# One SBUF operand in the small VectorE operations of softmax and norm, and other places for the second eviction tiles, in a two-layer streaming encoder

## The chip, the core and the metric

The kernel runs on one core of a Trainium2 chip. Its engines are TensorE (PE, matmuls, with weight loads as PEld), VectorE (DVE), ScalarE (ACT), GpSimd (POOL) and SyncE (SP), from whose queue all DMAs are issued. The metric is the device time of one execution in microseconds; lower is better. Before the change it is 2810.72 us, the median of three runs (2810.69 to 2818.3).

## The reference

One inference step of a two-layer encoder over 1152 rows of width 1024: a prompt of 1024 positions and 8 samples of 16. Layer 0 uses sliding-window attention with grouped keys, a learned sink per head and a relative-position bias; layer 1 uses chunk-band attention with keys and values shared by all B layers. Cut to what the change touches:

```python
# attention of layer 0, with sinks: the sink joins the maximum and the sum
m = jnp.maximum(s.max(-1, keepdims=True), sink)
e = jnp.exp(s - m)
p = e / (e.sum(-1, keepdims=True) + jnp.exp(sink - m))
o = jnp.einsum('bkgqs,bskd->bqkgd', p.astype(v.dtype), v)
...
# after the attention and after the channel mixer of each layer
x = layer_norm(DEEPNORM_ALPHA * x + (1 + g_m) * mix, ln_g[l, 0], ln_b[l, 0])
f, conv_rows = conv_ffn(h, ...)          # causal convolution, GEGLU, down-projection
x = layer_norm(DEEPNORM_ALPHA * x + (1 + g_f) * f, ln_g[l, 1], ln_b[l, 1])
...
def layer_norm(x, g, b):
    mu = x.mean(-1, keepdims=True)
    var = jnp.square(x - mu).mean(-1, keepdims=True)
    return (x - mu) * lax.rsqrt(var + LN_EPS) * g + b
```

## The kernel before, in words

Matmul operands are kept as a high and a low part (fp32r), so a product takes three passes; `split` (line 167 the cast on ACT, line 178 the subtraction on DVE or POOL) makes the two parts. The rows stand as 9 token tiles of 128 (tile 8 holds the samples). The program is: `opening`, `attention(0)`, `out_proj(0)`, `ffn(0)` with `down`, then the same for layer 1, whose attention begins with `kv`. A scheduler sets the order of the instructions on each engine from the order in which the program writes them and its own timeline; within an engine they then run strictly in that order. Waits between engines are on semaphores, derived from which parts of a tile are written and read.

The large SBUF tile F is used again and again: in each stage an arena hands out pieces of it. In `attention(0)` these are, by column, the softmax results (7328 to 9888), the bias tiles (to 10400), the transposed weights `pTs` of the sample items (10400 to 10784), `osm`, `rl`, then `L` (11040, the sums of the exponentials), `M` (11168, the negated maxima), `ost` and `pitem` (from 11808). At the same time the K and V projections of the attention's start still use F for the second eviction tiles: `kstore` and `vtile` evict a result once as high and low part into X2 and, for the last rows that are outputs, once more in plain form into a tile of the ring `kvt`, 384 columns each, from which a DMA stores it (line 371 for V). Before the change these tiles lie at 10368, 10752, 11136, 11520, 11904 and 12288. V is computed for the token tiles 0, 1, 2, 8, 3, 4, 5, 6, 7 in this order; tile 7 gets the ring's third tile, at 11136.

For each head and pair of query tiles, `scores` lets PE form the scores (lines 540 and 543) and `softmax` adds the bias and takes the minimum of the negated scores with an accumulator output in `M` (line 507, on DVE), then exponentiates on ACT with the sum into `L` (line 511). `weigh` transposes the weights on PE (568), `sums` adds the sink's share to `L` and inverts (lines 612 to 614), `values` multiplies with V (590) and `normalise` scales on POOL (628). Between them lie the query projections (296), pieces of the adaLN projections (224, with weights loaded by line 216), and the sample items: scores (682), a softmax that adds the sink's share in line 699, transposes (708), values (717), a scaling on DVE (725) and a transpose back (730). Near the end, `ocast` and `woload` put splits of 1024 columns on ACT and POOL (lines 167 and 178).

In the norms, `rsqrt` refines the inverse root by a Newton step: lines 967, 968 and 969 are operations on one column of 128 rows. `norm_tail` closes the first three norms, and POOL multiplies by the gain there (line 1039). `norm_last` closes the last one: for token tiles in `VT` two operations on DVE apply mean, gain, root and shift (993, 994); for the others ACT applies mean and root (996, 997), POOL the gain (998) and DVE the shift (999). In the last stage the tiles are finished in the order 0, 1, 2, 6, 7, 8, 3, 4, 5, so tile 5 is the last of the program.

## Time and profile before

| | us |
|---|---|
| median of three runs | 2810.72 |
| profiled execution | 2808.31 |
| its span, from the first to the last instruction | 2806.5 |
| PE busy in the span | 2701.0 |
| DVE busy | 1898.8 |
| ACT busy | 1307.8 |
| POOL busy | 1117.7 |
| mean granted TensorE clock | 0.987 |

The first attention lies from about 84 to 390 us of the span, its output projection until about 500, the channel mixer of layer 0 and its norm until about 1270, K, V and the attention of layer 1 from there to about 1900, and the last channel mixer ends the program. In a timeline row the columns are start in us, length in us (of all the instructions merged in the row), engine, line, operation, out<-in, and in brackets the idle time before it with what ended it. In a row of stretches each engine has its busy time and its count in the order PE, PEld, DVE, ACT, POOL, and then come the granted TensorE clock (1.00 is full), the share of DMA time and GB/s. SPq is the DMA queue on SyncE: the length there is that of issuing.

### The profile page before, as it was taken

What the parts mean: (1) busy time and instruction counts of PE and PEld (TensorE: products, weight loads), DVE (VectorE), ACT (ScalarE), POOL (GpSimd) and SP (SyncE); (2) the same over time, 40 slices, a digit from 0 to 9 for tenths busy, and PEclk for the clock granted to TensorE, in tenths of its full rate; (3) what the DMA queues carried; (4) which work ended last, traced back from release to release, by engine and by line L of the source; (5) the groups of instructions that cost most, each with busy time, mean ns of one, the idle gap of its engine ahead of it and who ended that gap; (6) DMA issues with size and microseconds to landing.
All of it is one profiled execution on the core that took longest, in us unless ns stands there. A gap on an engine that the chain in (4) does not pass through costs nothing.

```text
span 2806.5 us, 46569 instructions
## 1 busy us (share of the span) xinstructions
PE 2701.0 (96%) x17398; PEld 2384.3 (85%) x17398; DVE 1898.8 (68%) x3622; ACT 1307.8 (47%) x2607; POOL 1117.7 (40%) x755
## 2 busy tenths in 40 slices
PE   7999889999999999999999999989999999999997
PEld 5897768989999998777898888867899999998886
DVE  4376768776666684766854667766887777774764
ACT  3375633533333343443536666663444444444442
POOL 2132523444333457565220121242444333458662
PEclk9999999999999999999999999999999999999999
DMA  7656434474444446665757457763432222247662
GB/s 291 212 157 198 146 98 173 146 250 142 143 156 145 142 132 220 214 225 195 266 199 268 120 153 192 221 202 122 170 123 71 72 80 71 71 143 256 210 199 76
DMA packets 205187, 467.96 MB, mean 167 GB/s; under 512 B 34752, under 2 KB 97936, under 8 KB 204960
## 3 DMA queue, kind: packets, MB, share of 16 engines
q1 hardware_dynamic: 204960, 464.98, 51.0%
q8 instruction: 137, 2.24, 0.3%
q14 instruction: 90, 0.74, 0.1%
HBM read 365.17 MB, written 109.17 MB: 169 GB/s over the span
## 4 chain that ended last, share of the span: by engine, by line
PE 40%; DVE 4%; DMA 3%; ACT 2%; issue 1%; POOL 0%; SPq 0%; POOLq 0%; DVEq 0%; ACTq 0%
PE PS L1203 18%; PE PS L1386 10%; PE PS L296 4%; PE PS L309 4%; PE PS L590 1%; PE PS L568 1%; PE PS L540 1%; DVE F L507 1%; DMA F<-hmD 1%; PE PS L543 1%; ACT F L919 1%; PE PS L717 0%; DVE wl L178 0%; DMA F<-hD 0%; DVE xa L178 0%
## 5 line engine op out<-in xcount | busy, mean ns | idle before, releaser
L1203 PE MATMUL PS<-H,wh 128*128 128x320 f32 (+1 forms) x2752 | 427.9, 298 | 0.0
L1203 PEld LDWEIGHTS PS<-H,wh 128*128 128x128 f32 x2752 | 390.3, 192 | 0.4 <-issue 0.4
L1164 DVE TENSOR_TENSOR F<-PS,F 128x256 f32<-128x256 f32 (+1 forms) x446 | 197.7, 453 | 199.7 <-PE PS L1203 198.9
L167 ACT CAST wh<-F 128x512 fp32r<-128x512 f32 (+3 forms) x265 | 168.0, 645 | 328.3 <-PE PS L1203 186.6
L1379 DVE TENSOR_TENSOR xa<-xa 128x384 fp32r<-128x384 f32 x132 | 180.8, 1379 | 190.5 <-ACT xa L167 189.0
L1250 DVE SCALAR_TENSOR_TENSOR F<-F 128x1024 f32<-128x1024 f32 x320 | 258.9, 855 | 4.5 <-ACT F L1289 3.4
L178 DVE TENSOR_TENSOR wl<-F,wh 128x512 fp32r<-128x512 f32 (+2 forms) x236 | 215.0, 924 | 61.9 <-ACT wh L167 61.5
L1203 PE MATMUL PS<-H,wl 128*128 128x320 f32 (+1 forms) x1376 | 244.0, 300 | 8.7 <-ACT F L1171 7.2
L296 PE MATMUL PS<-H,wh 128*128 128x384 f32 (+1 forms) x1152 | 225.1, 339 | 0.0
L1386 PE MATMUL PS<-wh,xa 128*128 128x512 f32 x696 | 222.0, 395 | 0.0
L178 POOL TENSOR_TENSOR wl<-ws,wh 128x1024 fp32r<-128x1024 f32 x59 | 148.6, 2523 | 178.8 <-ACT wh L167 144.1
L1203 PEld LDWEIGHTS PS<-H,wl 128*128 128x128 f32 x1376 | 205.1, 192 | 16.9 <-ACT F L1171 7.7
L1203 PE MATMUL PS<-xa,wh 128*128 128x320 f32 (+1 forms) x1408 | 216.6, 296 | 1.4 <-DVE xa L178 1.4
L167 ACT CAST wh<-ws 128x512 fp32r<-128x512 f32 (+1 forms) x159 | 126.8, 804 | 190.8 <-PE PS L1203 94.8
L296 PEld LDWEIGHTS PS<-H,wh 128*128 128x128 f32 x1152 | 200.9, 189 | 1.3 <-issue 0.8
L1203 PEld LDWEIGHTS PS<-xa,wh 128*128 128x128 f32 x1408 | 197.4, 189 | 2.1 <-DVE xa L178 1.7
L1259 POOL TENSOR_TENSOR F<-F 128x16 f32<-128x16 f32 x88 | 47.8, 543 | 312.4 <-DVE F L1250 220.5
L1386 PEld LDWEIGHTS PS<-wh,xa 128*128 128x128 f32 x696 | 130.6, 188 | 30.7
L167 ACT CAST xa<-xa 128x384 fp32r<-128x384 f32 x132 | 67.4, 513 | 187.6 <-DMA xa<-actD 181.9
L309 PE MATMUL PS<-wh,H 128*128 128x512 f32 (+1 forms) x576 | 145.7, 367 | 1.4 <-DVE F L1095 0.8
L628 POOL TENSOR_TENSOR F<-F,X 64x512 f32<-64x512 f32 x62 | 79.5, 1282 | 169.6 <-DVE F L604 147.7
L1297 POOL TENSOR_TENSOR F<-F 128x1152 f32<-128x1152 f32 x44 | 119.8, 2722 | 49.5 <-DVE F L1250 31.3
(269 smaller groups left out, 6193.0 us busy)
## 6 DMA issues: line engine op xcount, KB each, us to landing
ws<-in_wdn_dram SPq DMA_DIRECT2D x66, 512.0 KB
F<-in_wdn_dram SPq DMA_DIRECT2D x66, 512.0 KB
ws<-in_adaw_dram SPq DMA_DIRECT2D x64, 512.0 KB
actD<-F SPq DMA_DIRECT2D x44, 576.0 KB
xa<-actD SPq DMA_DIRECT2D x132, 192.0 KB
ws<-in_wup_dram SPq DMA_DIRECT2D x49, 512.0 KB
F<-in_adaw_dram SPq DMA_DIRECT2D x48, 512.0 KB
F<-in_wup_dram SPq DMA_DIRECT2D x39, 512.0 KB
```

Source lines behind the costliest of these rows:

```text
L167: nc.scalar.copy(out, in_)
L178: self.eng(el).tensor_sub(lo, src, hi.bitcast(F32))
L296: mm = self.nc.tensor.matmul(out[:, 0:n], w[a][:, k * 128 : k * 128 + 128], H[:, p, k, s0 : s0 + n], start=i == 0, stop=i == 23)
L309: self.nc.tensor.matmul(out[:, 0:n], H[:, p, j * kn + k, t0 : t0 + 128], w[a][:, k * n : k * n + n], start=i == 0, stop=i == 23,)
L628: self.eng("v" if last else "p").tensor_mul(on[r, q], on[r, q], rb[r, :])
L1164: nc.vector.tensor_add(d, v(ps), a if len(a.shape) == 3 else v(a))
L1203: self.pairmm = nc.tensor.matmul(ps[:, 0:m], w[a][:, k * 128 : k * 128 + 128], x(p, k, n), start=start and c == 0, stop=c == 11, skip_grou ...
L1250: nc.vector.scalar_tensor_tensor(o, u, cw[:, cc, i : i + 1], o, op0=ALU.mult, op1=ALU.add)
L1259: nc.gpsimd.tensor_add(y3[:, :, 0:2], y3[:, :, 0:2], E4[:, cc])
L1297: nc.gpsimd.tensor_mul(yg, yg, ya)
L1379: nc.vector.tensor_sub(lo, raw, hi.bitcast(F32))
L1386: self.downmm = nc.tensor.matmul(ps, a[p][:, i * 128 : i * 128 + 128], w[q][:, hf * 512 : hf * 512 + 512], start=j == 0 and c == 0, stop=j ...
```

## The change

`M` and the part of `L` that takes the sums become one tile `LM` with two columns per query tile, the sum and the negated maximum side by side. `sums` reduces each such pair into `L` with one tensor_reduce, which has one SBUF operand, where it added two tiles. In the sample items' softmax and in `rsqrt` and `norm_last`, products and sums of two columns are written as tensor_scalar: one tensor operand and one column as a scalar per row. The second eviction tiles get fixed places: 9120, 9504, 11520, 11904, 12288 and 10400, in the ring's order. Token tile 5 joins `VT`. No other line changes, but two lines more in the file put the lines after 412 one or two further down: line 507 is 508 then, 613 is 615, 699 is 701, 969 is 971, and 993 to 999 are 995 to 1001.

```diff
-VT = (0, 3, 6, 7)
+VT = (0, 3, 5, 6, 7)
...
         L = fa.take(128)
-        M = sa.take(128) if l == 0 else None
+        LM = fa.take(256).rearrange("p (i t) -> p i t", t=2) if l == 0 else None
...
-        ka = Arena(self.F, 10368 if l == 0 else 0)
-        kvt = Ring([(self.X2[:, i * 768 : i * 768 + 768], ka.take(384)) for i in (0, 3, 1, 4, 2, 5)])
+        late = (9120, 9504, 11520, 11904, 12288, 10400)
+        late = [self.F[:, o : o + 384] if l == 0 else None for o in late]
+        kvt = Ring([(self.X2[:, i * 768 : i * 768 + 768], f) for i, f in zip((0, 3, 1, 4, 2, 5), late)])
...
-                nm = M[:, i : i + 1] if l == 0 else self.sm.next()[:, 0:1]
-                softmax(pieces, p, n, self.sink[:, h : h + 1] if l == 0 else None, nm, L[:, i : i + 1])
+                nm = LM[:, i, 1:2] if l == 0 else self.sm.next()[:, 0:1]
+                rs = LM[:, i, 0:1] if l == 0 else L[:, i : i + 1]
+                softmax(pieces, p, n, self.sink[:, h : h + 1] if l == 0 else None, nm, rs)
...
             if l == 0:
-                nc.scalar.activation(M[:, cs], M[:, cs], AF.Exp, bias=self.sinkH[:, hh : hh + 1])
-                nc.vector.tensor_add(L[:, cs], L[:, cs], M[:, cs])
+                nc.scalar.activation(LM[:, cs, 1], LM[:, cs, 1], AF.Exp, bias=self.sinkH[:, hh : hh + 1])
+                nc.vector.tensor_reduce(out=L[:, cs], in_=LM[:, cs, :], op=ALU.add, axis=mybir.AxisListType.X)
             nc.vector.reciprocal(L[:, cs], L[:, cs])
...
                 nc.scalar.activation(e, sink, AF.Exp, bias=nm, scale=-1.0)
-                nc.vector.tensor_add(rs, rs, e)
+                nc.vector.tensor_scalar_add(rs, rs, e)
             nc.vector.reciprocal(rs, rs)
...
         nc.vector.tensor_scalar(t, t, -0.5, 1.5, op0=ALU.mult, op1=ALU.add)
-        nc.vector.tensor_mul(r, r, t)
+        nc.vector.tensor_scalar_mul(r, r, t)
...
         else:
-            nc.vector.tensor_mul(m, s, r)
+            nc.vector.tensor_scalar_mul(m, s, r)
```

What stands on DVE at the first softmax of the program, before (PS is PSUM, F, C and xa are SBUF tiles, DMAHW0 to 7 the semaphores of the DMA queue; the rows of line 494 are the low parts of the query projection):

```order
L494 SCALAR_TENSOR_TENSOR xa<-PS,xa 64x256 [waits PE_49,Activation_49]
L507 ISA F<-PS,F,C 128x128 [waits DMAHW0_49,DMAHW1_49,PE_49,Pool_49]
L507 ISA F 128x1
L494 SCALAR_TENSOR_TENSOR xa<-PS,xa 64x256 [waits Activation_49]
L507 ISA F<-PS,F,C 128x256 [waits PE_49,Pool_49]
```

And after:

```order
L495 SCALAR_TENSOR_TENSOR xa<-PS,xa 64x256 [waits PE_49,Activation_49]
L508 ISA F<-PS,F,C 128x128 [waits DMAHW0_49,PE_49,Pool_49]
L508 ISA F 128x1
L495 SCALAR_TENSOR_TENSOR xa<-PS,xa 64x256 [waits Activation_49]
L508 ISA F<-PS,F,C 128x256 [waits PE_49,Pool_49]
```

The order is the same; the first softmax no longer waits for one of its two DMAs.

In the attention the small operations keep their places and waits. On DVE, a piece near the end of the first attention (lines 699 and 700 the sample items' sum and inverse, 739 their eviction, 613 and 614 those of the prompt), before:

```order
L699 TENSOR_TENSOR C<-C 128x1 [waits Activation_49]
L739 COPY F<-PS 64x4x16 [waits PE_49]
L739 COPY F<-PS 64x4x16
L613 TENSOR_TENSOR F<-F 128x4 [waits DVE_49,Activation_49]
L700 RECIPROCAL C<-C 128x1 [waits DVE_49]
```

And after:

```order
L701 TENSOR_SCALAR C<-C 128x1 [waits Activation_49]
L741 COPY F<-PS 64x4x16 [waits PE_49]
L741 COPY F<-PS 64x4x16
L615 TENSOR_REDUCE F<-F 128x4 [waits DVE_49,Activation_49]
L702 RECIPROCAL C<-C 128x1 [waits DVE_49]
```

Only the form of two rows differs: one tensor operand, where there were two.

The last rows of DVE, the norm of token tile 5, before (986 and 990 prepare mean and variance, 965 to 969 the inverse root):

```order
L990 TENSOR_SCALAR C<-C 128x1 [waits Activation_49]
L965 RECIPROCAL C<-C 128x1 [waits Activation_49]
L967 TENSOR_SCALAR C<-C 128x1 [waits DVE_49]
L968 TENSOR_SCALAR C<-C 128x1 [waits DVE_49]
L969 TENSOR_TENSOR C<-C 128x1 [waits DVE_49]
L996 TENSOR_TENSOR C<-C 128x1 [waits DVE_49]
L999 TENSOR_TENSOR F<-F 128x1024 [waits Pool_49]
```

And after:

```order
L992 TENSOR_SCALAR C<-C 128x1 [waits Activation_49]
L995 SCALAR_TENSOR_TENSOR F<-F,C 128x1024 [waits DVE_49]
L967 RECIPROCAL C<-C 128x1 [waits Activation_49]
L969 TENSOR_SCALAR C<-C 128x1 [waits DVE_49]
L970 TENSOR_SCALAR C<-C 128x1 [waits DVE_49]
L971 TENSOR_SCALAR C<-C 128x1 [waits DVE_49]
L996 SCALAR_TENSOR_TENSOR F<-F,C 128x1024 [waits DVE_49]
```

The wait for POOL at the end is gone, and with it one operation of 1024 columns on ACT and one on POOL; DVE has two in place of one, the first of them ahead of the inverse root. Elsewhere the scheduler exchanges some neighbours: on all engines at the starts of the two channel mixers and in `kv`, a few matmuls in the output projections.

## Prediction

> **What bounds the kernel now.** I read the page's busy times and chain first, then the waits of VectorE (DVE) by line over the first attention, then the timeline wherever TensorE (PE) stands idle in it, with the granted clock beside it.

> ```profile
> PE 2701.0 (96%) x17398; PEld 2384.3 (85%) x17398; DVE 1898.8 (68%) x3622; ACT 1307.8 (47%) x2607; POOL 1117.7 (40%) x755
> PE 40%; DVE 4%; DMA 3%; ACT 2%; issue 1%; POOL 0%; SPq 0%; POOLq 0%; DVEq 0%; ACTq 0%
> ```

> PE is busy for 96% of the span and carries most of the chain that is traced. So a change on DVE is worth only what it takes out of PE's idle time, or out of time at a lower clock, or out of the end, after the last matmul. Elsewhere it is free. The edit touches three kinds of places.

> **Part 1: the eviction tiles.** Waits of DVE and timelines of the DMA queue, DVE and PE where the first softmax stands (columns: start in us, length in us, engine, line, then in brackets the idle time before and what ended it), and two stretches with the clock (the number before the DMA share):

> ```profile
> DVE F L507 <- DMA out_va_dram<-F: 6.1, 1, 6.1
> ...
> 99.91 0.53 SPq L366 DMA_DIRECT2D vH<-X  x1
> 100.90 0.34 SPq L371 DMA_DIRECT2D out_va_dram<-F  x1
> 106.79 1.00 SPq L471 DMA_DIRECT2D xa<-vH  x2
> 107.88 2.00 SPq L216 DMA_DIRECT2D ws<-in_adaw_dram  x2
> ...
> 100.72 0.42 DVE L494 SCALAR_TENSOR_TENSOR xa<-PS,xa 64x256 fp32r<-64x256 f32 x1 [2.26 <-ACT xa L493]
> 107.26 0.35 DVE L507 CUSTOM_DVE_ANT_0 F<-PS,F,C 128x128 f32<-128x128 f32 x1 [6.12 <-DMA out_va_dram<-F]
> ...
> 107.67 0.38 PE L540 MATMUL PS<-xa 128*128 128x256 f32 x1 [2.73 <-DVE F L507]
> 110.91 0.58 PE L540 MATMUL PS<-xa 128*128 128x256 f32 x1 [1.16 <-DVE F L507]
> ...
> 110.00:117.00 7.00, 6.09 (x22) 6.09 (x23) 4.39 (x17) 4.21 (x15) 0.00 (x0) 0.51 0.70 229
> 117.00:120.00 3.00, 3.00 (x22) 3.00 (x21) 0.75 (x3) 0.78 (x3) 0.00 (x0) 1.00 0.00 0
> ```

> Column 0 of M, the first thing that the first softmax writes, lay at F 11168, inside the tile 11136 to 11392 that holds the V rows of token tile 7 until they are stored. DVE therefore stood 6.12 us for that store. After the change the tile is at 11520 and the wait is gone from the row of the instruction. DVE can go on when L494 ends, at 101.14. PE loses its waits of 2.73 and 1.16, together 3.9 us. Behind the idle time the clock was 0.51 for 7 us. PE was busy 6.09 us of that, so a full clock would give 6.09 x 0.49 = 3.0; I take 2.6, as part of it is short dependent matmuls. What is late next: the V load of L471 still leaves at 106.79, because it reads what the store at 99.91 writes, and the loads of L216 stand behind it in the same queue. All of them have landed by 117 (DMA share 0.00 from there), so PE, 6.5 us earlier, may meet the second one; I take off 1.0. The tiles' new places also overlap pitem and pTs, but these are first used by the items (L699 below, from 189.4), long after the stores. Part 1: 3.9 + 2.6 - 1.0 = 5.5 us, between 0 (all given back to those loads) and 7.

> **Part 2: the small operations.** Rows by line (shortest, median and longest in ns), a control in the norms, and the end of the first attention:

> ```profile
> L613 DVE TENSOR_TENSOR F<-F x32: 140/164/2321, 115.1 to 371.7; 128x4 f32<-128x4 f32 x32
> L699 DVE TENSOR_TENSOR C<-C x16: 128/159/3328, 189.4 to 385.0; 128x1 f32<-128x1 f32 x16
> L969 DVE TENSOR_TENSOR C<-C x36: 104/160/2374, 415.2 to 2797.5; 128x1 f32<-128x1 f32 x36
> L968 DVE TENSOR_SCALAR C<-C x36: 129/153/156, 415.0 to 2797.3; 128x1 f32<-128x1 f32 x36
> L614 DVE RECIPROCAL F<-F x64: 155/178/180, 115.3 to 1887.0; 128x4 f32<-128x4 f32 x64
> ...
> 437.81 2.38 POOL L1039 TENSOR_TENSOR F<-F 128x1024 f32<-128x1024 f32 x1 [11.02 <-DVE C L965]
> 438.31 0.26 DVE L967 TENSOR_SCALAR C<-C 128x1 f32<-128x1 f32 x1
> 438.61 0.15 DVE L968 TENSOR_SCALAR C<-C 128x1 f32<-128x1 f32 x1
> 438.80 1.42 DVE L969 TENSOR_TENSOR C<-C 128x1 f32<-128x1 f32 x1
> 410.00:440.00 30.00, 30.00 (x140) 24.57 (x139) 28.65 (x60) 6.15 (x15) 8.99 (x4) 1.00 0.34 123
> ...
> 329.20 2.34 POOL L178 TENSOR_TENSOR H<-H 128x1024 fp32r<-128x1024 f32 x1
> 328.22 3.33 DVE L699 TENSOR_TENSOR C<-C 128x1 f32<-128x1 f32 x1
> 331.48 0.33 DVE L725 TENSOR_SCALAR F<-PS,C 128x128 f32<-128x128 f32 x1
> 331.87 0.46 PE L730 MATMUL PS<-C,F 128*128 128x128 f32 x1 [3.04 <-DVE F L725]
> 332.00:349.00 17.00, 14.20 (x89) 10.29 (x89) 13.01 (x39) 11.29 (x29) 10.89 (x8) 0.60 0.16 54
> ...
> 290.68 2.32 DVE L613 TENSOR_TENSOR F<-F 128x4 f32<-128x4 f32 x1 [0.21 <-ACT F L612]
> 288.00:295.00 7.00, 7.00 (x55) 6.65 (x48) 6.54 (x15) 6.49 (x18) 3.69 (x2) 1.00 0.46 133
> ```

> The same operation takes 160 ns or up to 3328 ns. At 437.81 GpSimd (POOL) begins a multiply of 2.38 us. Two operations with one SBUF tensor, L967 and L968, run inside it at their usual 0.26 and 0.15 us; L969, with two SBUF operands, ends at 440.22, where the multiply ends (440.19). So it is the second SBUF operand that waits for POOL. The new forms have one: L699 and L969 become the form of L968 (150 ns, never above 156), L613 a reduction that no row shows. By its neighbours it lies between L614's 178 ns on the same four columns and, as an end far away, the 3328 ns above; I take 0.18 us, the nearest row.

> [...]

> What it is worth: L699 at 328.22 loses 3.33 - 0.16 = 3.2 us, L725 behind it starts that much earlier, and with it PE's 3.04. In the 17 us behind, the clock is 0.60 with PE busy for 14.20, which holds 14.20 x 0.40 = 5.7 us; DVE is busy for 13.01 of the same stretch, so I take half, 2.9. Some small idle gaps of PE there belong to later waits of the same two lines; I put 1.1 on those. Part 2 in the attention: 7 us, between 3 (the 3.04 alone) and 11 (the whole 5.7 and 2 more). [...]

> I cost the rest at nothing: L613's 2.32 at 290.68 lies beside a PE that is busy for 7.00 of 7.00, L969's beside 30.00 of 30.00. That cover is PE work in front of the waiting result; if it were gone, each would show its own one or two microseconds. L996 was short each time. The extra cost of the new forms, some 20 ns each, is below what matters.

> **Part 3: token tile 5 in VT.** It is the last tile of the program. Tile 3, already on the other branch, shows what it will do:

> ```profile
> 2778.90 0.15 DVE L990 TENSOR_SCALAR C<-C 128x1 f32<-128x1 f32 x1 [1.31 <-ACT F L989]
> 2778.97 1.28 DVE L993 SCALAR_TENSOR_TENSOR F<-F,C 128x1024 f32<-128x1024 f32 x1
> 2781.05 1.28 DVE L994 SCALAR_TENSOR_TENSOR F<-F,C 128x1024 f32<-128x1024 f32 x1
> ...
> 2796.39 0.15 DVE L990 TENSOR_SCALAR C<-C 128x1 f32<-128x1 f32 x1 [1.31 <-ACT F L989]
> 2797.96 1.24 ACT L997 ACTIVATE F<-F,C 128x1024 f32<-128x1024 f32 x1 [1.18 <-DVE C L996]
> 2799.28 2.34 POOL L998 TENSOR_TENSOR F<-F 128x1024 f32<-128x1024 f32 x1 [6.93 <-ACT F L997]
> 2801.65 1.23 DVE L999 TENSOR_TENSOR F<-F 128x1024 f32<-128x1024 f32 x1 [3.79 <-POOL F L998]
> ```

> From L990 to the end of the row: 2802.88 - 2796.39 = 6.49 us before; in tile 3, 2782.33 - 2778.90 = 3.43. The first of the two operations lies beside the square root, and nothing else is left on DVE. Part 3: 3.0 us, between 2.5 and 3.1. The store of the last row follows as before.

> **Sum.** 5.5 + 7 + 3.0 = 15.5 us. The profiled execution took 2808.31 us (2806.5 of it the span), so 2792.8; the median of the runs shown, 2810.72, stands 2.4 above it, so 2795.2 on that scale. I say 2794. The bounds add up to 5.5 and 21, that is about 2787 to 2805.

> **Rivals.**

> Given back. PE's start in the attention moves, but the next thing in line was late anyway: the weight loads of L216, V of L471, or, at the end, the reloads and normalisations that run through SyncE's queue. For it, the waits of PE from 100 to 400 us:

> ```profile
> PE PS L224 <- DMA ws<-in_adaw_dram: 7.1, 7, 1.3
> ```

> Against: the queue's rows shift with PE, since those loads wait for buffers that PE frees. Then part 3 and about a third of the rest stay: 2808.3 - 7 = 2801.

> The small forms wait all the same. The control row speaks against it for L699 and L969, nothing does for the reduction. Then parts 1 and 3 are left: 2808.3 - 8.5 = 2800.

> The tile is moved in vain: the first softmax meets another transfer, such as its bias, in place of the store. Against it, POOL's fill of the first bias tile had its load at 99.61:

> ```profile
> 99.61 0.14 POOL L520 MEMSET F<- 64x64 f32 x1 [17.10 <-DMA F<-ska]
> ```

> Parts 2 and 3: 2798.

> Slower: the reduction is dear. It stands 32 times in the attention, each in front of the reciprocal and a later softmax. If it costs 1.0 us in place of 0.18 on PE's path, 32 x 0.82 = 26 us are added: 2808.3 - 15.5 + 26 = 2819. It decides from some 0.75 us each, where the saving is used up and 8 more are lost. For it only that no row shows the form; against it the nearest row, L614's 178 ns. [...]

> **How the numbers follow.** Forecast 0.60; given back 0.17; forms wait 0.10; moved in vain 0.07; slower 0.06. What a measurement can tell from no change is 0.3%, 8.4 us: faster means below 2802.3. The forecast and the vain move lie there (0.67), half of the cases at 2800 and 2801 just so, with the 2 us between the two scales in mind (0.05 of 0.10 and 0.05 of 0.17). Faster 0.77, within 0.17, slower 0.06. The range reaches from 2783, the bounds with a little more clock, to 2806, where part 3 alone is left and what was given back is nearly all.

> **What would show it.** Part 1: the first softmax (L508 then) starts near 101, with no wait for the V store, and the clock stays at 1.00 from 110 to 117. Part 2: none of L615, L701, L971 is longer than 0.3 us; the matmul of L732 waits no 3 us; the clock between 325 and 345 has less time at one half. Part 3: the last operation of DVE is the second of two of 1.28 us, 3.4 us behind L992. The forecast is wrong if PE's idle time in the attention is the same as before in sum, at other lines, or if the starts of the channel mixers, where the casts on ScalarE (ACT) stand in a slightly different order now, hold PE up longer than this wait, the longest one from 2050 to 2080 us:

> ```profile
> PE PS L1203 <- ACT F L1171: 4.3, 1, 4.3
> ```

## The result, and the profile after

| | before | after |
|---|---|---|
| median, us (6 runs each, side by side) | 2810.94 (2808.1 to 2818.3) | 2794.45 (2791.05 to 2801.12) |
| ratio of the two | | 0.9938, 95% interval 0.9921 to 0.9956 |
| profiled execution, us | 2808.31 | 2793.26 |
| its span, us | 2806.5 | 2791.5 |
| mean granted clock in it | 0.987 | 0.989 |

The kernel is 16.5 us faster in the medians and 17.4 by the ratio, with an interval of 12 to 22; the forecast was 2794. In a second comparison on another occasion (the run `all_again` below) the same kernel was 10.1 us faster by the ratio, 6.7 to 13.8. That difference matters for what follows: the forecast met the time, but its three terms did not all hold, and the experiments tell which.

The page of the changed kernel, busy time and the chain's shares:

```profile
PE 2696.8 (97%) x17398; PEld 2382.1 (85%) x17398; DVE 1898.6 (68%) x3622; ACT 1305.3 (47%) x2606; POOL 1112.6 (40%) x754
PE 41%; DVE 4%; DMA 3%; ACT 2%; issue 1%; SPq 0%; POOL 0%; DVEq 0%; ACTq 0%; POOLq 0%
```

PE bounds the kernel as before. Its busy time fell by 4.2 us though it executes the same 17398 matmuls, and the time at half clock, summed over the span from the windows in the trace's record of the clock, fell from 71.6 to 62.5 us.

The first softmax, from the timeline of the changed kernel, and the stretch with the clock that was 0.51 before:

```profile
101.06 0.35 DVE L508 CUSTOM_DVE_ANT_0 F<-PS,F,C 128x128 f32<-128x128 f32 x1
110.00:117.00 7.00, 7.00 (x57) 5.89 (x56) 4.49 (x17) 4.19 (x15) 0.29 (x2) 1.00 0.51 183
```

The small operations by line (shortest, median and longest in ns; L970 is the old L968 and did not change):

```profile
L615 DVE TENSOR_REDUCE F<-F x32: 138/161/163, 109.7 to 361.9; 128x4 f32<-128x8 f32 x32
L701 DVE TENSOR_SCALAR C<-C x16: 184/210/215, 181.5 to 375.2; 128x1 f32<-128x1 f32 x16
L971 DVE TENSOR_SCALAR C<-C x36: 160/214/218, 408.5 to 2786.2; 128x1 f32<-128x1 f32 x36
L970 DVE TENSOR_SCALAR C<-C x36: 129/154/156, 408.3 to 2786.0; 128x1 f32<-128x1 f32 x36
```

None of them waits for POOL any more, where the longest of the old ones took 2321, 3328 and 2374 ns. And the waits of PE in the first attention (95 to 395 us) that the prediction spoke of, with the longest one at the last channel mixer:

```profile
PE PS L224 <- DMA ws<-in_adaw_dram: 7.7, 5, 2.5
...
PE PS L732 <- DVE F L727: 0.3, 1, 0.3
...
PE PS L1205 <- ACT F L1173: 5.8, 1, 5.8
```

PE's wait of 3.04 in front of the sample items' transpose back is 0.3. The last rows of DVE:

```profile
2784.22 0.15 DVE L992 TENSOR_SCALAR C<-C 128x1 f32<-128x1 f32 x1 [1.31 <-ACT F L991]
2784.30 1.27 DVE L995 SCALAR_TENSOR_TENSOR F<-F,C 128x1024 f32<-128x1024 f32 x1
...
2786.43 1.28 DVE L996 SCALAR_TENSOR_TENSOR F<-F,C 128x1024 f32<-128x1024 f32 x1
```

From L992 to the end is 2787.71 - 2784.22 = 3.49 us, where it was 6.49.

So every sign that the prediction named appeared. But if one instruction after another is matched between the two traces, the lead over before is not the sum of the three terms in their places: 7.9 us at 190 us, only 1.3 to 3.2 between 265 and 310, 9.8 at 369, 6.6 at 490, and from there it drifts to 12 before the tail (why was not followed). In this pair of traces the lead of the first term is lost again by 265 us. The middle of it is seen in the stretch from 200 to 260 us, of before and then of after:

```profile
200.00:260.00 60.00, 54.74 (x491) 43.20 (x489) 39.12 (x142) 36.05 (x107) 14.25 (x15) 1.00 0.67 203
```

```profile
200.00:260.00 60.00, 52.62 (x434) 41.67 (x433) 34.99 (x131) 33.59 (x102) 14.83 (x15) 0.91 0.64 187
```

PE is busy for 2.1 us less there after the change, at a clock of 0.91 where it was 1.00, and executes 57 fewer matmuls. What it waits for is above all the weights of the adaLN projections (L224 above). One pair of traces cannot tell whether the tiles bring this about; the section on the parts alone comes back to it.

### The profile page after: what moved, and what is told of

Read it like the earlier page. It is cut to its first block, busy times and chain, and to the rows that moved or that the text cites. A ratio compares the mean times of both kernels' runs of the same rounds, so it can differ in the third digit from the quotient of the medians.

```text
span 2791.5 us, 46560 instructions
## 1 busy us (share of the span) xinstructions
PE 2696.8 (97%) x17398; PEld 2382.1 (85%) x17398; DVE 1898.6 (68%) x3622; ACT 1305.3 (47%) x2606; POOL 1112.6 (40%) x754
## 4 chain that ended last, share of the span: by engine, by line
PE 41%; DVE 4%; DMA 3%; ACT 2%; issue 1%; SPq 0%; POOL 0%; DVEq 0%; ACTq 0%; POOLq 0%
PE PS L1205 17%; PE PS L1388 10%; PE PS L296 5%; PE PS L309 3%; PE PS L592 2%; PE PS L570 2%; DMA F<-hmD 1%; PE PS L541 1%; ACT F L921 1%; DVE F L508 1%; PE PS L544 1%; PE PS L719 0%; DVE wl L178 0%; DMA ws<-in_wo_dram 0%; DVE F L606 0%
## 5 line engine op out<-in xcount | busy, mean ns | idle before, releaser
L1381 DVE TENSOR_TENSOR xa<-xa 128x384 fp32r<-128x384 f32 x132 | 193.1, 1475 | 184.7 <-ACT xa L167 180.1
L178 DVE TENSOR_TENSOR wl<-F,wh 128x512 fp32r<-128x512 f32 (+2 forms) x236 | 221.8, 951 | 56.0 <-ACT wh L167 55.6
L178 POOL TENSOR_TENSOR wl<-ws,wh 128x1024 fp32r<-128x1024 f32 x59 | 150.3, 2552 | 184.6 <-ACT wh L167 152.0
L309 PE MATMUL PS<-xa,H 128*128 128x512 f32 x504 | 132.9, 405 | 6.2 <-ACT xa L167 3.3
```

Of the source, the lines that this page charges most:

```text
L178: self.eng(el).tensor_sub(lo, src, hi.bitcast(F32))
L309: self.nc.tensor.matmul(out[:, 0:n], H[:, p, j * kn + k, t0 : t0 + 128], w[a][:, k * n : k * n + n], start=i == 0, stop=i == 23,)
L1381: nc.vector.tensor_sub(lo, raw, hi.bitcast(F32))
```

## The experiments

Theory A is the prediction: the three parts are independent and add up. Theory B, formed from the two traces: the tiles' part is given back to the weight loads, and what the forms bring is one place, the sample items near 330 us. Each kernel ran beside the kernel before, whose median was 2806.76, 2808.41 and 2810.27 us in the three sets (25, 26 and 17 runs). A difference in us below is what the ratio makes of that median; the ratio is not simply the quotient of the two medians shown, and the two can lie some 2 us apart. None of the kernels leaves out work.

**The parts alone**

`tiles_only`, the kernel before with

```diff
-        ka = Arena(self.F, 10368 if l == 0 else 0)
-        kvt = Ring([(self.X2[:, i * 768 : i * 768 + 768], ka.take(384)) for i in (0, 3, 1, 4, 2, 5)])
+        late = (9120, 9504, 11520, 11904, 12288, 10400)
+        late = [self.F[:, o : o + 384] if l == 0 else None for o in late]
+        kvt = Ring([(self.X2[:, i * 768 : i * 768 + 768], f) for i, f in zip((0, 3, 1, 4, 2, 5), late)])
```

> The kernel before with the new places of the second eviction tiles and nothing else. Theory A (the prediction, parts add up): 5.5 us less than before, 2805.4 against 2810.9, and the lead is still there at the end of the first attention. Theory B (given back, as the trace of the changed kernel suggests, where a lead of 7.9 us at 132 to 216 us was 1.3 to 2.5 at 265 to 287): the first softmax starts near 101 us here too, but PE then waits more for the adaLN weights (line 224), and of the lead 1 to 2.5 us are left: 2808.4 to 2809.9. In the trace: the lead of the DVE instructions over before at 130, 215, 270, 390 and 2700 us.

`forms_only`, the kernel before with `LM`, the reduction and all four tensor_scalar forms of the diff.

> The kernel before with the small operations in their new forms (LM with the reduction, and all four tensor_scalar forms), eviction tiles and VT as before. Theory A: 7 us less, 2803.9, nearly all of it between 315 and 370 us of the span. Theory B (what these operations lost in waits for POOL outside that stretch was hidden by PE, but shorter queues on DVE also help later stages): 8 to 10 us, with 1 to 3 of them behind 400 us. Theory C (the new forms cost as much in their own time as they save): within 2 us of before.

`vt_only`, the kernel before with

```diff
-VT = (0, 3, 6, 7)
+VT = (0, 3, 5, 6, 7)
```

> The kernel before with token tile 5 in VT and nothing else. Theory A: 3.0 us less, 2807.9, all of it behind the last matmul: from the end of the last small operation of tile 5 to the end of the last DVE operation 3.4 us in place of 6.5. Rival: the two operations of 1.28 us wait behind tile 4's on DVE, and 1.2 us or more of the 3.0 are lost: 2809.

`all_again`, the changed kernel as it is.

> The changed kernel once more, for the spread between runs and for a second profile. Theory A (parts add up) and theory B (first part given back, others larger) both expect 2791 to 2801; what it tells is whether the windows at half clock at 210, 251 and 374 us are there again (then they belong to the kernel's own waits) or not (then they come and go from run to run, and part of the give-back is chance).

| kernel | median, us (runs) | ratio to before | us against before |
|---|---|---|---|
| tiles_only | 2808.53 (11) | 1.0003 (0.9994 to 1.0012) | +0.8 (-1.7 to +3.4) |
| forms_only | 2800.31 (9) | 0.9977 (0.9968 to 0.9987) | -6.5 (-9.0 to -3.6) |
| vt_only | 2806.36 (11) | 0.9991 (0.9980 to 1.0002) | -2.5 (-5.6 to +0.6) |
| all_again | 2797.83 (5) | 0.9964 (0.9951 to 0.9976) | -10.1 (-13.8 to -6.7) |

The parts add up within their intervals: 0.8 - 6.5 - 2.5 = -8.2, beside -10.1. But the tiles are worth nothing that can be measured, and 5.5 us is outside their interval. Theory A fails there and holds for the forms. The runs cannot tell `vt_only` from no change (by the two medians alone it is 0.4 us faster); its trace can: from the end of PE's last matmul to the end of DVE's last operation it is 8.07 us there, 11.12 before. Of the half-clock windows near 210, 251 and 374 us that the first trace after showed, the last two were there again in `all_again`, at 249 and 372, and the first stood at 229 (10.2 us of half clock between 130 and 300 us in both).

Why the tiles bring less than 5.5 us has one side that is clear. The first softmax of three kernels that have the old places, `forms_only`, `vt_only` and, from the next set, `norm_forms`:

```profile
104.05 0.35 DVE L507 CUSTOM_DVE_ANT_0 F<-PS,F,C 128x128 f32<-128x128 f32 x1 [3.12 <-DMA out_va_dram<-F]
```

```profile
105.18 0.35 DVE L507 CUSTOM_DVE_ANT_0 F<-PS,F,C 128x128 f32<-128x128 f32 x1 [2.84 <-DMA out_va_dram<-F]
```

```profile
106.93 0.35 DVE L507 CUSTOM_DVE_ANT_0 F<-PS,F,C 128x128 f32<-128x128 f32 x1 [4.49 <-DMA out_va_dram<-F]
```

The wait for the V store varies from profile to profile: 2.84, 3.12, 4.23, 4.49, 5.23 and 6.12 us in the six profiles with old places. The 6.12 from which the prediction worked is the largest. In the two with the shortest waits the clock never fell to one half between 95 and 130 us, so with them the 2.6 us of clock that the prediction added do not exist either. What theory B adds is that PE waits more for weights later. In `tiles_only`, from 95 to 395 us:

```profile
PE PS L224 <- DMA ws<-in_adaw_dram: 9.6, 9, 2.3
```

These waits are 7.1, 5.0, 6.9, 6.4, 7.0 and 7.9 us in the six profiles with old places (mean 6.7), and 9.6, 7.7, 7.0, 9.6, 6.5 and 6.4 in the six with new ones (mean 7.8). So they cost about 1.1 us more on average, with a spread that is larger.

The loss between 210 and 265 us in the pair before and after is for the most part no mark of the tiles. Matched matmul by matmul with the profile of before, `forms_only`, `vt_only` and `attn_forms` (of the next set), which keep the old places, are ahead by 6.0, 4.9 and 3.9 us at 210 us, `tiles_only` by 4.7. At 265 us the five other profiles with old places lie between 3.4 us ahead and 2.9 behind, and the six with new ones 0.8 to 4.2 ahead. All but one of these eleven have 3.4 to 10.2 us at half clock between 130 and 300 us; `dummy_two` has none, like before. So the profile of before has the longest wait of all at the first softmax, and no half clock in the 170 us from 130 on. In the means over six profiles each, the new places are 3.7 us ahead of the old at 210 us and 2.5 at 265.

Counting all idle time of PE from 95 to 300 us gives the same: the means are 10.0 us with the old places and 8.6 with the new ones; time at half clock there is 10.2 and 8.0 us, of which at most half is taken as lost, an estimate from the granted 0.5. That is 1.4 + 1.1, about 2.5 us, that the tiles bring by the profiles; by the runs they bring nothing, between a gain of 1.7 and a loss of 3.4. The two do not quite agree, and where the rest goes was not found: what is left of the predicted 5.5 is between nothing and about 2.5.

**Which of the forms**

`attn_forms` is the kernel before with `LM`, the reduction and line 699; `norm_forms` with

```diff
-        nc.vector.tensor_mul(r, r, t)
+        nc.vector.tensor_scalar_mul(r, r, t)
...
-            nc.vector.tensor_mul(m, s, r)
+            nc.vector.tensor_scalar_mul(m, s, r)
```

and, after the dummies below had been seen, `item_form` with one line:

```diff
-                nc.vector.tensor_add(rs, rs, e)
+                nc.vector.tensor_scalar_add(rs, rs, e)
```

> The kernel before with the two new forms of the attention alone (LM with the reduction, and the sample items' sum as tensor_scalar); norms, tiles and VT as before. Theory A (the prediction: all that the forms are worth lies in the first attention, the norms' waits are covered by PE): as much as all four forms together, 5 to 7 us less than before. Theory B (the norms' forms carry part of it, since shorter queues on DVE help later stages too): 3 to 4 us.

> The kernel before with the two new forms of the norms alone (the last product of the Newton step, and mean times root in the last norm). Theory A: 0, within 1.5 us of before, although some 20 us of waits for POOL go from DVE. Theory B: 2 to 3 us less.

> The kernel before with one line changed, the sample items' sum as tensor_scalar (16 instances); LM, reduction, norms, tiles and VT as before. Theory A (now: the gain of the forms is the one wait in front of the sample items' scaling near the end of the first attention, and the waits of the prompt's sums were covered, as the 32 added operations that waited 10 and 12 us for POOL and cost nothing suggest): as much as both forms of the attention together, 5 to 6.5 us less than before, with the clock at 0.85 or more from 330 to 360 us. Theory B (the reduction carries it): within 1.5 us of before, clock 0.65 to 0.76 there.

| kernel | median, us (runs) | ratio to before | us against before |
|---|---|---|---|
| attn_forms | 2802.93 (11) | 0.9982 (0.9968 to 0.9995) | -5.1 (-9.0 to -1.4) |
| norm_forms | 2809.32 (12) | 1.0003 (0.9990 to 1.0016) | +0.8 (-2.8 to +4.5) |
| item_form | 2800.32 (12) | 0.9963 (0.9949 to 0.9978) | -10.4 (-14.3 to -6.2) |

The norms' forms bring nothing, though some 20 us of waiting left DVE: PE covers them, as predicted. The one line of the sample items brings all that both forms of the attention bring; with 10.4 it came out above the 5 to 6.5 that was expected, but its interval reaches down to 6.2, and those of `attn_forms` and `forms_only` reach up to 9.0. The place is seen in the stretch 330 to 365 us. First two kernels with the old line 699, `tiles_only` and `norm_forms`, then two with the new one, `item_form` and `forms_only` (PE's busy time is the third number, the clock the third from the right):

```profile
330.00:365.00 35.00, 29.00 (x166) 21.16 (x167) 26.56 (x84) 21.30 (x58) 18.61 (x15) 0.61 0.20 63
```

```profile
330.00:365.00 35.00, 26.53 (x163) 18.77 (x164) 28.18 (x84) 21.56 (x60) 20.18 (x16) 0.67 0.23 77
```

```profile
330.00:365.00 35.00, 26.84 (x221) 18.57 (x220) 27.16 (x89) 23.01 (x65) 22.09 (x18) 0.85 0.24 80
```

```profile
330.00:365.00 35.00, 28.82 (x227) 20.64 (x228) 23.46 (x93) 22.02 (x64) 18.32 (x13) 0.90 0.21 70
```

The time at half clock in this stretch, summed from the windows in the trace's record of the clock:

| line 699 | kernels | us at half clock, 330 to 365 us |
|---|---|---|
| two SBUF operands | before, norm_forms, vt_only, tiles_only | 17.1, 23.3, 17.1, 27.0 |
| one, as tensor_scalar | item_form, attn_forms, forms_only, after, all_again, dummy_one, dummy_two, vt_four | 10.2, 6.8, 6.8, 10.2, 6.8, 8.8, 6.8, 6.8 |

The two groups do not overlap here; their means are 21.1 and 7.9 us. By an estimate from the granted 0.5, the 13.2 us between them cost at most half, 6.6; with PE busy for 27.5 of 35 us (the mean of the first group) it is 5.2. PE's wait in front of line 730 is 3.0, 3.0, 2.8 and 2.7 us in the first group. So by this stretch and that estimate the one wait of DVE, some 3 us, cost PE those 3 and about 5 more by the clock behind it. The clock's part depends on the bounds: from 300 to 405 us the sums are 17.1, 23.9, 23.9 and 41.0 us against 10.2 to 20.5, and the groups overlap. The time itself does not: matched matmul by matmul, the eight kernels with the new line gain 4.6 to 8.8 us on the profile of before between 328 and 369 us, while the other three of the first group lose 0.5 to 2.1.

**Does a second operand cost anything in the prompt's sums?**

`dummy_two` and `dummy_one` are the changed kernel with one added operation behind each of the 32 reductions, on two SBUF operands and on one:

```diff
                 nc.vector.tensor_reduce(out=L[:, cs], in_=LM[:, cs, :], op=ALU.add, axis=mybir.AxisListType.X)
+                nc.vector.tensor_add(LM[:, cs, 1], LM[:, cs, 1], LM[:, cs, 0])
```

```diff
                 nc.vector.tensor_reduce(out=L[:, cs], in_=LM[:, cs, :], op=ALU.add, axis=mybir.AxisListType.X)
+                nc.vector.tensor_scalar_add(LM[:, cs, 1], LM[:, cs, 0], 1.0)
```

> The changed kernel with one more operation behind each of the 32 reductions: a tensor_tensor with two SBUF operands on 4 columns, whose result nobody reads. Theory A (a second SBUF operand waits for POOL and holds up the later softmaxes on DVE): the added operations take up to 2.3 us where POOL is at work, and 3 to 7 us come back, 2800.5 to 2805. Rival (the gain of the forms has another cause, such as where LM lies): as the kernel with 32 one-operand operations, within 1.5 us of it.

> The changed kernel with one more operation behind each of the 32 reductions: a tensor_scalar with one SBUF operand on 4 columns and a constant, whose result nobody reads. Theory A: none of them longer than 0.3 us, 32 x 0.16 = 5 us more on DVE, beside PE for the greater part: 0 to 1.5 us above the changed kernel (2797.8). Rival (any operation more on DVE there costs its time): 3 to 5 us above it.

`dummy_two` took 2797.19 us (6 runs; ratio 0.9968, 0.9956 to 0.9979, that is 9.0 us less than before), `dummy_one` 2798.81 (7 runs; 0.9966, 0.9953 to 0.9978, 9.5 less), beside 10.1 less for the changed kernel without them. (The scheduler also puts about a hundred matmuls, 35 of them in the first attention, a little earlier or later when the operations are added, in the same way for both.) Neither costs anything that can be measured, and the two cannot be told apart: the 3 to 7 us that theory A expected back with `dummy_two` did not come. The lines of the added operations, of `dummy_two` and of `dummy_one`:

```profile
L616 DVE TENSOR_TENSOR F<-F x32: 142/164/1952, 110.4 to 360.2; 128x4 f32<-128x4 f32 x32
```

```profile
L616 DVE TENSOR_SCALAR F<-F x32: 147/172/3209, 110.1 to 361.4; 128x4 f32<-128x4 f32 x32
```

Both wait for POOL, 10 us in sum and 12. That the second does was expected by neither theory: it has one SBUF operand. One place of `dummy_one`:

```profile
137.21 0.16 DVE L615 TENSOR_REDUCE F<-F 128x4 f32<-128x8 f32 x1
137.26 1.29 POOL L631 TENSOR_TENSOR F<-F,X 64x512 f32<-64x512 f32 x1 [3.05 <-DVE F L606]
137.41 1.17 DVE L616 TENSOR_SCALAR F<-F 128x4 f32<-128x4 f32 x1
138.49 0.16 DVE L617 RECIPROCAL F<-F 128x4 f32<-128x4 f32 x1
```

POOL's multiply ends at 138.55 and the tensor_scalar on 4 columns at 138.58. So the count of SBUF operands alone does not decide. In these traces a tensor_scalar on one column ran through (of 36 instances of L971 in the trace after, 13 lay wholly inside one operation of POOL and none took more than 218 ns), a tensor_scalar on 4 columns waited (up to 3209 ns), and so did one on 1024 (L1008 in the norms takes 806 to 2647 ns in the trace after, and the eight instances above 1 us end 0.55 us behind the end of an operation of POOL); the reduction of 4 x 2 columns ran through (12 of 32 inside one operation of POOL, none above 163 ns). What decides between them is not shown: the one-column operations also lie in tile C and the wider ones with both sides in SBUF in F, so the number of columns was not separated from the tile.

That the medians see nothing of these 10 and 12 us fits what `item_form` says: in the prompt's part of the attention most of such waits lie beside PE's own work. At least one of the 32 does not. In `dummy_one`:

```profile
326.22 3.21 DVE L616 TENSOR_SCALAR F<-F 128x4 f32<-128x4 f32 x1
...
329.86 0.71 PE L685 MATMUL PS<-F 128*32 128x144 f32 x8 [3.19 <-DVE F L508]
```

PE waits 3.19 us for the softmax behind the added operation, and 2.02 us at the same place in `dummy_two`. So this one place cost PE two or three microseconds that the medians did not show. The sum with two operands does the same in the profile of `vt_only`:

```profile
325.09 2.35 POOL L178 TENSOR_TENSOR H<-H 128x1024 fp32r<-128x1024 f32 x1
...
326.46 3.86 DVE L613 TENSOR_TENSOR F<-F 128x4 f32<-128x4 f32 x1
327.41 0.32 POOL L274 TENSOR_TENSOR C<-C 128x72 f32<-128x72 f32 x1
327.70 0.30 POOL L275 TENSOR_TENSOR C<-C 128x72 f32<-128x72 f32 x1
327.97 2.33 POOL L178 TENSOR_TENSOR H<-H 128x1024 fp32r<-128x1024 f32 x1
330.96 0.71 PE L682 MATMUL PS<-F 128*32 128x144 f32 x8 [3.86 <-DVE F L507]
```

The sum waits through four operations of POOL that follow one another without a gap, until 330.32, and PE waits 3.86 us for the softmax behind it. `item_form` has the same (4.12 us, and as long on PE) in its own profile, which is the slowest of its 12 runs (2809.3 us). So with line 699 alone the exposed wait can come back a few instructions earlier; how often it does was not measured, and the medians cannot tell the reduction's share from zero. The profiles of before, `norm_forms` and `tiles_only`, which have the old sum too, show no wait of this length there.

**The tiles without the adaLN loads**

`late_ada_old` is the kernel before with the background projections moved from the first attention to behind it, and `late_ada_tiles` the same with the new places. Between the two the order of the instructions is the same on every engine.

```diff
-        self.bg = [self.ada(1, 4), self.ada(2, 4)]
         self.attention(0)
+        self.bg = [self.ada(1, 4), self.ada(2, 4)]
```

> The kernel before with the background adaLN projections (lines 224 and 216) moved from the inside of the first attention to behind it; nothing left out, tiles, forms and VT as before. It is the base for the next kernel. PE has less to fill its gaps with in the attention, so it should be 5 to 40 us slower than before; no theory hangs on that. The first softmax should wait for the V store here too, 2.8 to 6.1 us.

> The same with the new places of the second eviction tiles. Theory A (without the adaLN weights, for which PE waits in line 224, nothing takes the tiles' lead back): 3 to 6 us less than the kernel with the old places. Theory B (the lead is lost whatever follows, as other waits or the clock take it): within 1.5 us of it.

They took 2879.13 us (4 runs, 2877.33 to 2884.66) and 2870.43 (5 runs, 2867.53 to 2874.0): the first move costs 71 us, more than expected, and the tiles give 8.7, also more. Their first softmaxes:

```profile
104.22 0.48 DVE L507 CUSTOM_DVE_ANT_0 F<-PS,F,C 128x256 f32<-128x256 f32 x1 [5.94 <-POOL wl L178]
```

```profile
101.00 0.48 DVE L508 CUSTOM_DVE_ANT_0 F<-PS,F,C 128x256 f32<-128x256 f32 x1 [1.91 <-POOL F L522]
```

The trace does not bear out theory A as it stood. The wait in the first is not put down to the V store but to POOL. The lead is 3.2 us at 104 and 1.7 from 110 to 210, 0 from 220 to 250 and between 1.5 and 3.5 from 270 to 400, and so it is not taken back for good here; but most of the rest of the 11.7 us by which the two profiled runs differ appears near 410 us and between 1900 and 1940, where the tiles are no longer in use. The time at half clock in the two is 184.6 and 147.4 us, which by the same estimate can be worth up to half the difference, 18.6. Why that differs between two kernels of the same order is open, and with it how much of the 8.7 us belongs to the tiles.

**A version that goes further**

```diff
-VT = (0, 3, 5, 6, 7)
+VT = (0, 3, 4, 5, 6, 7)
```

> The changed kernel with token tile 4 in VT as well. Theory A: the addition of 1.22 us for tile 4 (line 1001) no longer stands on DVE ahead of tile 5's last norm, and its two operations of 1.28 us lie before 2779 us, where DVE waits for PE: 1.1 us less than the changed kernel, all behind the last matmul, 4.1 less there than before. Rival: they come in the way of tile 5's additions and 0 to 1.3 us are lost. The runs' medians can't tell 1 us; the trace's last 10 us can.

`vt_four` took 2792.0 us (6 runs, 2790.08 to 2797.18), ratio to before 0.9943 (0.9926 to 0.9960). From the end of PE's last matmul to the end of DVE's last operation it is 11.12 us before, 8.13 in the changed kernel and 7.17 here, so 0.96 of the expected 1.1 are there. Its last rows:

```profile
2786.59 0.15 DVE L988 TENSOR_SCALAR C<-C 128x1 f32<-128x1 f32 x1
2788.11 0.15 DVE L992 TENSOR_SCALAR C<-C 128x1 f32<-128x1 f32 x1 [1.37 <-ACT F L991]
2788.18 1.27 DVE L995 SCALAR_TENSOR_TENSOR F<-F,C 128x1024 f32<-128x1024 f32 x1
...
2790.31 1.28 DVE L996 SCALAR_TENSOR_TENSOR F<-F,C 128x1024 f32<-128x1024 f32 x1
```

The addition of tile 4 that stood for 1.22 us ahead of L988 is gone. It has the lowest median of all, but the changed kernel's ratio in the first comparison was 0.9938, and 1 us between the two is less than the runs can tell.

## Why the prediction was right, and where it was not

**Part 1, the eviction tiles (5.5 us, 0 to 7): the step that failed.** The mechanism was there: the first softmax starts at 101.06 us, without the store, and the clock stays at 1.00 from 110 to 117. But the term that was taken, 3.9 of waiting and 2.6 of clock (the author's estimate, in place of the 3.0 worked out from the granted clock), came from the longest of six waits (2.84 to 6.12 us): in place of 6.5 the profiles show 3.7 us on average at 210 us. Of that 1.2 are lost by 265 us, about the 1.0 that was taken off for the weight loads; PE's waits for them are 1.1 us longer on average, and they come several times until 250 us and not once. That makes 2.5 where 5.5 was forecast. Measured alone it is +0.8 us (-1.7 to +3.4), so even this is not confirmed by the runs. The rival "given back" comes nearest for this part, but that the loads take the whole of it back is not shown.

**Part 2, the small operations (7 us, 3 to 11): right in size and place, wrong in its rule.** The forms brought 6.5 us (3.6 to 9.0), by the one place that the prediction named. Of the terms, the wait of 3.04 is confirmed; the clock behind it was taken as 2.9 and is about 5 by the profiles from 330 to 365 us, less surely in a wider stretch, and the 1.1 of small gaps was not seen apart. That the rest of the waits costs nothing holds for the norms (`norm_forms`). For the prompt's sums it holds in the medians of the two dummies, but four profiles (`vt_only`, `item_form` and the dummies) have one place each where such a wait cost PE 2.0 to 4.1 us. The reduction at 161 ns is near the 0.18 us that was taken, below the reciprocal on the same columns with its 178 ns, and the rival "reduction dear" is out (its limit of some 0.75 us does not follow from its own numbers: (15.5 + 8) / 32 above 0.18 is about 0.9). The sentence "it is the second SBUF operand that waits for POOL" is too narrow: a tensor_scalar on 4 columns with one SBUF operand waits as well (up to 3209 ns in `dummy_one`). The rival "the small forms wait all the same" fails for the forms that were written (none above 218 ns); of a tensor_scalar over 4 columns behind the prompt's sums it is true, as `dummy_one` has it. The extra cost, put at 20 ns, is 50 to 60 ns where the second operand became a scalar per row (L701 210 for 159, L971 214 for 160), some 3 us of DVE in all, without effect.

**Part 3, the tail (3.0 us, 2.5 to 3.1): right by the traces.** 6.49 to 3.49 in the changed kernel and 3.44 in `vt_only`. The runs of `vt_only`, with -2.5 us (-5.6 to +0.6), allow it but do not show it.

**The sum.** With the terms as measured it is 0 + 6.5 + 3.0 = 9.5, up to 12 if the profiles' 2.5 for the tiles counts; three kernels with all parts (`all_again` and the two dummies) were 10.1, 9.0 and 9.5 us faster than before, `vt_four` 16.0 (11.2 to 20.8). The comparison that the forecast was made for gave 16.5, or 17.4 by the ratio like the others. There the kernel before had a median of 2810.9 in 6 runs, while in the later sets it had 2806.8, 2808.4 and 2810.3; the changed kernel's own medians, 2794.45 and 2797.83, lie 3.4 us apart. That the forecast met 2794 to half a microsecond is therefore partly luck: a term that was 3 to 5.5 us too high stood against a comparison in which the change came out some 7 us larger than in the next one. Why the sets differ by that much is not settled; the later ones ran on two different chips. The forecast "faster" does not depend on it.

The starts of the channel mixers, named as a risk, did not decide: the wait in front of the last one is 5.8 us where it was 4.3.

## What to carry to other kernels

A wait that one profile shows is one sample: before its length becomes a term, look whether it ends on a transfer (the one here was waited for 2.84 to 6.12 us in six profiles) or on an engine's own instruction, and ask which queue of loads PE meets next if it comes earlier. In the one case here a short idle gap of PE cost its length, some 3 us, and, with the halved clock behind it, by estimate about 5 us more, so the first gap to look at is one in a stretch whose granted clock is low (0.61 and 0.67 from 330 to 365 us in the two rows above with the old line); the many waits of DVE beside a busy PE were worth nothing that could be measured here (`norm_forms`, +0.8 us, -2.8 to +4.5). A lead between two traces is only a hint: before it is put down to the change, match other traces of the kernel without the change too, as they may show the same lead and the same loss. To keep small VectorE work out of GpSimd's way, look at the shape too and not only at the number of operands: here one column as tensor_scalar (at most 218 ns), or a reduction (at most 163 ns), ran through, and a tensor_scalar on four columns in SBUF did not (up to 3209 ns).
